# A hybrid decoder layer on one core: gates from plain one-hot columns, and mixers on four pairs of tiles

## The chip, the core and the metric

The kernel runs on one core of a Trainium2 chip. The metric is device time in microseconds (us). The kernel before took 3249.86 us, the median of 3 runs (3240.8 to 3261.46). Five engines work side by side: PE (TensorE, matmuls; its weight loads are listed apart as PEld), DVE (VectorE), ACT (ScalarE), POOL (GpSimd) and SP (SyncE, which issues most transfers). Each works through its own list of instructions in order and waits on semaphores for the others. Data moves between HBM and the on-chip SBUF by DMA; matmul results land in PSUM.

## The reference

One layer over 1024 tokens of 1024 features, all in float32, in four steps:

```
h = x
h += W_out [ norm(attn) ; norm(conv) ]     # token mixers: both from norm(h) @ w_in
h += PEER(norm(h))                         # 8 heads x 16 of 128*128 experts per token
h += sigmoid(norm(h) @ W_g) * (p @ W_p)
return norm(h)

# PEER, for a block of 128 tokens: eb = expert numbers (i1*128 + i2), gb = softmax gates
h   = einsum('td,tkd->tk', xb, expert_u[eb])
act = gelu(h) * gb
y   = einsum('tk,tkd->td', act, expert_v[eb])
```

Attention has 8 heads of 64 under three dilated causal patterns, the convolution 31 taps over 512 channels. The search for experts takes the 16 best of 128 keys on each of two sides, then the 16 best sums, for each token and head: 128 slots a token.

## The kernel before

**Tiles and groups.** The 1024 tokens are 8 tiles of 128. GROUPS cuts them into five groups: tile 0, then (1, 2), (3, 4), (5, 6), then tile 7. For each group the kernel streams all mixer and search weights once (22 MB a group): stage_in projects q, k, v; stage_attend does attention and the convolution; stage_out normalises, projects with w_out and adds the residual; stage_search projects PEER queries and finds the top keys on DVE; stage_combine finds the top sums, the gates and the expert numbers. The loop near the end of tile_layer interleaves the stages of neighbouring groups. In matmuls with channels on the partitions (channel_major) the moving operand is as wide as the group: 128 or 256 columns; in those with tokens on the partitions (token_major) each tile costs the same in any group.

**The convolution** (convolve) splits its taps: 16 go through ACT (a scaled copy, `tap`) and POOL (an add, `side`), 15 through DVE (`cc`).

**Two ways through PEER.** Four tiles (FEW: 0, 1, 2, 7) gather: for each of 128 slots, POOL issues an indirect DMA that brings each token's row of expert_u (512 KB in all) into one of 6 buffers, DVE multiplies and sums it (`hk`); then the same with expert_v (`gy`). That is 256 rows of 512 KB a tile, 1024 in all, and they run in the background of everything else. The other four tiles (ALL: 3, 4, 5, 6) are dense: after the mixers, dense walks all 16384 experts in 128 column blocks, 32 groups of 4, with hi/lo split float32 matmuls (`ph`, `py`), and needs for each token a dense row of gates.

**The gate matrix.** gate_matrix builds those rows. For each token the slots' i1, i2 and gate stand on 128 partitions, and a matmul of two one-hot matrices, one of them scaled by the gates, gives 128 x 128 gates. For each 8 tokens DVE makes `o1` (128 keys x 8 tokens, bf16), for each 4 tokens `o2` (128 keys x 4 tokens), both with the tokens innermost; the scaling is one POOL multiply for the first four tokens (`ob`) and four ACT copies for the second four (`oa`). PE multiplies (`pG`), reading columns at a stride of 4; ACT copies PSUM to `stage`, SP writes 2 MB pieces to DRAM (`gate_d`). Each float32 matmul shows as two records on PE.

**What sets the order.** A scheduler in the framework writes each engine's list in advance; gathers, which come last in the program, are placed where it sees room. Buffers decide the rest: the dense stage's v and al tiles lie where the mixers' pool was, so they wait for the last stage_combine.

## Time and profile before

| what | us |
|---|---|
| median of 3 runs | 3249.86 |
| lowest and highest run | 3240.8, 3261.46 |
| the profiled execution | 3265.54 |
| its span, first to last instruction | 3263.7 |

The profiled execution is one run, 15.7 us above the median; 1.8 us of it lie outside the span. Its stages, as the trace shows them: mixers and search from 0 to 1103 us, the gate matrix from 1103 to 1413, the last search's combine to 1444, the dense stage to about 3034, the dense tiles' last step to 3154, then the last gathers and the last tile's last step to 3264. In the rows further down, a time in a list of instructions is the start in us from the span's start, followed by the duration; "mean ns" is the mean duration of one instruction. A duration is longer than the step to the next instruction of the same engine, since neighbours overlap a little.

### The profile page before, as it was taken

The page shows a single profiled execution, that of the slowest core. Times are in us where ns is not written, and L with a number is a line of the kernel's source. Part 1 is how long each engine was busy: PE and PEld are TensorE (multiplying, and loading weights), DVE is VectorE, ACT ScalarE, POOL GpSimd, SP SyncE. Part 2 cuts the span into 40 slices and gives each one's busy share as a digit, 9 for nine tenths or more (in the row PEclk, how much of TensorE's full clock was granted, in tenths as well). Part 3 has the DMA queues.
Part 4 walks back from the last instruction along what each step waited for, and adds up shares of the span by engine and source line. Part 5 has one row for each costly group of instructions (what it writes and reads, how often), then busy time and mean ns, then how long its engine had stood idle before and what let it go on. Part 6 is the DMA issues. An engine that isn't in the chain of part 4 may idle for free.

```text
span 3263.7 us, 37043 instructions
## 1 busy us (share of the span) xinstructions
PE 2814.0 (86%) x11843; PEld 2126.9 (65%) x11843; DVE 2633.1 (81%) x5226; ACT 1198.8 (37%) x2180; POOL 1650.2 (51%) x1392
## 2 busy tenths in 40 slices
PE   6697898899797599978999999899999997999952
PEld 3454375476366399965777777577777775777621
DVE  3379789889989766686888888778988886889895
ACT  4445326335525467752222222322222223222321
POOL 1247646353544443324565556545655554555673
PEclk9898999899899699989999999999999999999976
DMA  6575982684495363369999999989999998999895
GB/s 204 177 277 192 345 327 100 219 326 146 130 340 179 135 232 144 154 241 330 345 347 339 324 335 331 340 300 339 335 336 328 335 318 318 329 350 330 323 344 199
DMA packets 299989, 901.47 MB, mean 276 GB/s; under 512 B 27866, under 2 KB 94834, under 8 KB 297746
## 3 DMA queue, kind: packets, MB, share of 16 engines
q0 software_dynamic: 147456, 536.94, 45.6%
q1 hardware_dynamic: 149072, 358.81, 31.3%
q10 hardware_dynamic: 3266, 3.36, 0.3%
q8 instruction: 93, 1.52, 0.2%
q14 instruction: 102, 0.84, 0.1%
HBM read 857.06 MB, written 41.94 MB: 275 GB/s over the span
## 4 chain that ended last, share of the span: by engine, by line
PE 33%; DVE 25%; DMA 16%; issue 15%; POOL 8%; ACT 3%; ACTq 0%; POOLq 0%; SPq 0%; DVEq 0%
PE pG L674 7%; DMA v<-in_expert_v_dram 5%; POOL v L593 4%; DVE cc L356 4%; DVE gy L622 3%; DMA v<-in_expert_v_dram,ex 3%; DVE u L606 3%; PE py L760 2%; PE py L762 2%; PE py L761 2%; PE pq L270 2%; DVE ul L707 2%; POOL u L593 2%; PE o L261 2%; PE kept_y L760 2%
## 5 line engine op out<-in xcount | busy, mean ns | idle before, releaser
L593 POOL DMA_INDIRECT u<-in_expert_u_dram,ex x512 | 672.9, 1314 | 679.3 <-DVE hk L606 428.2
L593 POOL DMA_INDIRECT v<-in_expert_v_dram,ex x512 | 663.6, 1296 | 552.3 <-DVE gy L622 381.1
L622 DVE SCALAR_TENSOR_TENSOR gy<-v,ga,gy 128x1024 f32<-128x1024 f32 x512 | 663.8, 1296 | 50.3 <-DMA v<-in_expert_v_dram,ex 41.8
L606 DVE CUSTOM_DVE_ANT_0 u<-u,gxn 128x1024 f32<-128x1024 f32 x512 | 613.8, 1230 | 33.6 <-DMA u<-in_expert_u_dram,ex 32.3
L731 PE MATMUL ph<-xh,ul 128*128 128x512 f32 x1024 | 407.6, 398 | 24.9 <-DVE ul L707 24.5
L729 PE MATMUL ph<-xh,uh 128*128 128x512 f32 x1024 | 404.1, 395 | 14.8 <-ACT uh L705 14.8
L730 PE MATMUL ph<-xl,uh 128*128 128x512 f32 x1024 | 403.8, 394 | 0.0
L747 ACT CAST vh<-v 128x1024 fp32r<-128x1024 f32 x128 | 131.5, 1049 | 645.3 <-PE py L762 420.5
L350 POOL TENSOR_TENSOR side<-side,tap 128x256 f32<-128x256 f32 (+1 forms) x300 | 216.9, 724 | 174.1 <-ACT tap L349 152.6
L760 PE MATMUL py<-vh,ah 128*128 128x512 f32 x640 | 257.4, 403 | 51.9 <-ACT ah L739 51.9
L270 PE MATMUL pq<-x2T,w_pq 128*128 128x256 f32 (+1 forms) x1280 | 247.6, 343 | 12.4 <-ACT xt L286 5.7
L761 PE MATMUL py<-vl,ah 128*128 128x512 f32 x640 | 255.1, 401 | 0.0
L762 PE MATMUL py<-vh,al 128*128 128x512 f32 x640 | 253.7, 403 | 0.0
L731 PEld LDWEIGHTS ph<-xh,ul 128*128 128x128 f32 x1024 | 194.1, 190 | 79.5 <-DVE ul L707 37.6
L270 PEld LDWEIGHTS pq<-x2T,w_pq 128*128 128x128 f32 x1280 | 214.9, 195 | 36.1 <-ACT xt L286 6.1
L729 PEld LDWEIGHTS ph<-xh,uh 128*128 128x128 f32 x1024 | 194.2, 190 | 57.7 <-ACT uh L705 15.0
L749 DVE TENSOR_TENSOR vl<-v,vh 128x1024 fp32r<-128x1024 f32 x128 | 155.1, 1221 | 88.2 <-ACT vh L747 85.9
L730 PEld LDWEIGHTS ph<-xl,uh 128*128 128x128 f32 x1024 | 193.9, 189 | 43.6 <-issue 2.4
L705 ACT CAST uh<-u 128x1024 fp32r<-128x1024 f32 x128 | 134.4, 1050 | 135.2 <-PE ph L730 93.3
L760 PEld LDWEIGHTS py<-vh,ah 128*128 128x128 f32 x640 | 122.0, 191 | 90.7 <-ACT ah L739 64.6
L663 POOL TENSOR_TENSOR ob<-o,gT 128x512 f32<-128x512 bf16 x64 | 96.6, 1509 | 165.2 <-PE pG L674 142.1
L739 ACT CAST ah<-gelu 128x512 fp32r<-128x512 f32 x128 | 79.2, 620 | 273.3 <-DVE gelu L737 270.4
(262 smaller groups left out, 5358.4 us busy)
## 6 DMA issues: line engine op xcount, KB each, us to landing
u<-in_uT_dram SPq DMA_DIRECT2D x128, 512.0 KB
v<-in_expert_v_dram SPq DMA_DIRECT2D x128, 512.0 KB
w_pq<-in_peer_wq_dram SPq DMA_DIRECT2D x80, 512.0 KB
gate_d<-stage SPq DMA_DIRECT2D x16, 2048.0 KB
gt<-gate_d SPq DMA_DIRECT2D x64, 512.0 KB
w_o<-in_w_out_dram SPq DMA_DIRECT2D x40, 512.0 KB
we<-in_w_ple_gate_dram SPq DMA_DIRECT2D x24, 512.0 KB
w_k<-in_w_qkv_dram SPq DMA_DIRECT2D x20, 512.0 KB
```

The source lines that it names most:

```text
L270: nc.tensor.matmul(a, w[:, k, :], xT[:, k, :], start=k == 0, stop=k == KD - 1)
L350: G.tensor_tensor(side, side, m, ALU.add)
L593: d = G.indirect_dma_start(out=e, out_offset=None, in_=table, in_offset=bass.IndirectOffsetOnAxis(ap=index, axis=0))
L606: uses(V.tensor_tensor_reduce(out=e, in0=e, in1=xn, scale=1.0, scalar=0.0, op0=ALU.mult, op1=ALU.add, accum_out=hk[:, k : k + 1]))
L622: uses(V.scalar_tensor_tensor(y, e, act[:, k : k + 1], y, ALU.mult, ALU.add))
L674: nc.tensor.matmul(pg[:, rows(e)], o2[:, :, e], parts[e], start=True, stop=True)
L729: nc.tensor.matmul(ph, hi, xh[:, k, :], start=k == 0, stop=False)
L730: nc.tensor.matmul(ph, hi, xl[:, k, :], start=False, stop=False)
L731: nc.tensor.matmul(ph, lo, xh[:, k, :], start=False, stop=k == KD - 1)
L760: nc.tensor.matmul(py, ah[e][:, rows(j)], vh[e][:, half(f)], start=first, stop=False)
L761: nc.tensor.matmul(py, ah[e][:, rows(j)], vl[e][:, half(f)], start=False, stop=False)
L762: nc.tensor.matmul(py, al[e][:, rows(j)], vh[e][:, half(f)], start=False, stop=last_e)
```

## The change

The groups become four pairs, (0, 1), (2, 3), (4, 5), (6, 7); the gathered tiles are now 0, 1, 6, 7 and the dense ones 2 to 5. In the gate matrix o1, ob and the iotas table go. o2 is laid out with each token's 128 columns side by side; and for each token one instruction compares the key numbers with i1 and multiplies by the gate, on DVE for even tokens and on POOL for odd ones. ACT no longer scales anything there. A scratch tile of rstd moves to the buffers t2, and the search results get a fourth buffer.

```diff
-GROUPS = ((0,), (1, 2), (3, 4), (5, 6), (7,))
+GROUPS = ((0, 1), (2, 3), (4, 5), (6, 7))
-VB = 3
+VB = 4
-FEW = (0, 1, 2, 7)
-ALL = (3, 4, 5, 6)
+FEW = (0, 1, 6, 7)
+ALL = (2, 3, 4, 5)
...
-            sq = junk(f"sqj_{name}_{j}") if junk else mpool.tile([P, D], BF16, tag="sqj", name=f"sqj_{name}_{j}")
+            sq = junk(f"sqj_{name}_{j}") if junk else mpool.tile([P, D], BF16, tag="t2", name=f"sqj_{name}_{j}", bufs=3)
...
-            for o in range(0, BT, TB):
+            for o in range(0, BT, 4):
                 t0 = b * BT + o
-                o1 = gp.tile([P, NK, TB], BF16, tag="o1", name=f"o1_{j}_{t0}", bufs=2)
-                V.tensor_tensor(o1, i1T[:, t0 : t0 + TB].unsqueeze(1).to_broadcast([P, NK, TB]), iotas, ALU.is_equal)
-                for h in range(0, TB, 4):
-                    o2 = gp.tile([P, NK, 4], F32, tag="o2", name=f"o2_{j}_{t0 + h}", bufs=2)
-                    i2s = i2T[:, t0 + h : t0 + h + 4].unsqueeze(1).to_broadcast([P, NK, 4])
-                    V.tensor_tensor(o2, i2s, iotas[:, :, 0:4], ALU.is_equal)
-                    pg = sps(f"pG{j}_{t0 + h}")
-                    t = t0 + h
-                    if h == 0:
-                        a = gp.tile([P, NK, 4], F32, tag="ob", name=f"ob{j}_{t}")
-                        G.tensor_tensor(
-                            a, o1[:, :, 0:4], gT[:, t : t + 4].unsqueeze(1).to_broadcast([P, NK, 4]), ALU.mult
-                        )
-                        parts = [a[:, :, e] for e in range(4)]
-                    else:
-                        parts = []
-                        for e in range(4):
-                            a = gp.tile([P, NK], F32, tag="oa", name=f"oa{j}_{t}_{e}", bufs=3)
-                            S.activation(a, o1[:, :, h + e], AF.Copy, scale=gT[:, t + e : t + e + 1])
-                            parts.append(a)
-                    for e in range(4):
-                        nc.tensor.matmul(pg[:, rows(e)], o2[:, :, e], parts[e], start=True, stop=True)
-                    S.copy(stage[:, :, o + h : o + h + 4], pg.rearrange("p (t i) -> p i t", i=NK))
+                o2 = gp.tile([P, 4, NK], F32, tag="o2", name=f"o2_{j}_{t0}", bufs=3)
+                V.tensor_tensor(
+                    o2, i2T[:, t0 : t0 + 4].unsqueeze(2).to_broadcast([P, 4, NK]),
+                    iota.unsqueeze(1).to_broadcast([P, 4, NK]), ALU.is_equal,
+                )
+                pg = sps(f"pG{j}_{t0}")
+                for e in range(4):
+                    t = t0 + e
+                    a = gp.tile([P, NK], F32, tag=f"oa{e % 2}", name=f"oa{j}_{t}", bufs=4)
+                    (G if e % 2 else V).tensor_scalar(a, iota, i1T[:, t : t + 1], gT[:, t : t + 1], ALU.is_equal, ALU.mult)
+                    nc.tensor.matmul(pg[:, rows(e)], o2[:, e, :], a, start=True, stop=True)
+                S.copy(stage[:, :, o : o + 4], pg.rearrange("p (t i) -> p i t", i=NK))
```

The scheduler writes new lists from this. On DVE, early in the gate matrix, the list of before is the first one below and that of the change the second (o are the one-hot tiles, oa the scaled ones, gy the gathered sums of expert_v, xn a normalised tile).

```order
L654 TENSOR_TENSOR o_0_24_7400<-i1T_7303,iotas 128x1024
L658 TENSOR_TENSOR o_0_24_7402<-i2T_7309,iotas 128x512
L622 SCALAR_TENSOR_TENSOR gy_19722<-v_108_20048,ga_19719,gy_19722 128x1024
L658 TENSOR_TENSOR o_0_28_7412<-i2T_7309,iotas 128x512
L654 TENSOR_TENSOR o_0_32_7430<-i1T_7303,iotas 128x1024
L658 TENSOR_TENSOR o_0_32_7432<-i2T_7309,iotas 128x512
```

```order
L653 TENSOR_TENSOR o_0_0_6468<-i2T_6461,cst 128x512
L458 SCALAR_TENSOR_TENSOR xn_6410<-h_6_6340,r_ffn_6407,g_ffn 128x1024
L458 SCALAR_TENSOR_TENSOR xn_6426<-h_7_6342,r_ffn_6407,g_ffn 128x1024
L661 TENSOR_SCALAR oa_0_6471<-cst,i1T_6455,gT_6465 128x128
L661 TENSOR_SCALAR oa_2_6477<-cst,i1T_6455,gT_6465 128x128
L653 TENSOR_TENSOR o_0_4_6484<-i2T_6461,cst 128x512
```

From there DVE's list repeats one o and two oa, 128 times, with nothing between; gathers, the last search and the dense input stand behind the whole gate matrix. In the list of before they were mixed in. And the first o now stands behind both output projections of the last group (rows h_6, h_7 are read by the xn above).

POOL's list at the same place, before and with the change:

```order
L663 TENSOR_TENSOR ob_88_7633<-o_0_88_7628,gT_7313 128x512
L663 TENSOR_TENSOR ob_96_7663<-o_0_96_7658,gT_7313 128x512
L593 DMA v_119_20081<-in_expert_v_dram,ex_1462 128x1024
L663 TENSOR_TENSOR ob_104_7691<-o_0_104_7686,gT_7313 128x512
L593 DMA v_120_20084<-in_expert_v_dram,ex_1462 128x1024
```

```order
L592 DMA v_97_19624<-in_expert_v_dram,ex_1845 128x1024
L592 DMA v_98_19627<-in_expert_v_dram,ex_1845 128x1024
L661 TENSOR_SCALAR oa_1_6474<-cst,i1T_6455,gT_6465 128x128
L661 TENSOR_SCALAR oa_3_6480<-cst,i1T_6455,gT_6465 128x128
L661 TENSOR_SCALAR oa_5_6490<-cst,i1T_6455,gT_6465 128x128
```

The 256 oa of POOL now follow each other without a gather between them.

The end of DVE's list, from the last scaling of a dense tile's output on, before and with the change (v_77 and v_56 are numbers of slots; the last slot is 127 in both):

```order
L804 SCALAR_TENSOR_TENSOR h_6_5846<-h_6_5846,r_fin_19328,g_fin 128x1024
L622 SCALAR_TENSOR_TENSOR gy_22338<-v_77_22571,ga_22335,gy_22338 128x1024
L622 SCALAR_TENSOR_TENSOR gy_22338<-v_78_22574,ga_22335,gy_22338 128x1024
L622 SCALAR_TENSOR_TENSOR gy_22338<-v_79_22577,ga_22335,gy_22338 128x1024
L622 SCALAR_TENSOR_TENSOR gy_22338<-v_80_22580,ga_22335,gy_22338 128x1024
```

```order
L792 SCALAR_TENSOR_TENSOR h_5_4678<-h_5_4678,r_fin_18937,g_fin 128x1024
L621 SCALAR_TENSOR_TENSOR gy_21947<-v_56_22117,ga_21944,gy_21947 128x1024
L621 SCALAR_TENSOR_TENSOR gy_21947<-v_57_22120,ga_21944,gy_21947 128x1024
L621 SCALAR_TENSOR_TENSOR gy_21947<-v_58_22123,ga_21944,gy_21947 128x1024
L621 SCALAR_TENSOR_TENSOR gy_21947<-v_59_22126,ga_21944,gy_21947 128x1024
```

51 gathered rows stood behind the last dense tile, now 72 do. Counted along DVE's list, 255 gathered rows stood ahead of the last combine's end, now 232; in between, in the dense stage, both lists hold 20 rows for each group of four column blocks, and 28 to 34 where a gathered tile's last step falls in.

## Rows read from the trace of the kernel before

**Rows 1.** The page: span, busy time of each engine, and the mean busy share of the 16 DMA engines in 40 equal slices (tenths).

```profile
span 3263.7 us, 37043 instructions
PE 2814.0 (86%) x11843; PEld 2126.9 (65%) x11843; DVE 2633.1 (81%) x5226; ACT 1198.8 (37%) x2180; POOL 1650.2 (51%) x1392
DMA  6575982684495363369999999989999998999895
```

**Rows 2.** Busy time by stretch: from:to in us, length, then busy us and number of instructions of PE, PEld, DVE, ACT, POOL, the granted PE clock (share of full speed), DMA share, GB/s.

```profile
0.00:170.00 170.00, 111.67 (x584) 77.02 (x584) 57.59 (x247) 75.16 (x179) 28.11 (x64) 0.90 0.59 193
170.00:300.00 130.00, 112.12 (x433) 68.00 (x434) 112.34 (x306) 72.38 (x161) 76.19 (x74) 0.93 0.63 224
300.00:569.00 269.00, 230.35 (x941) 153.04 (x939) 232.46 (x682) 117.47 (x242) 163.74 (x152) 0.93 0.72 262
569.00:850.00 281.00, 249.52 (x1050) 164.20 (x1050) 252.51 (x814) 122.54 (x244) 129.34 (x125) 0.93 0.59 212
850.00:1103.00 253.00, 185.60 (x842) 125.86 (x842) 227.76 (x698) 106.30 (x220) 107.75 (x126) 0.87 0.57 204
1103.00:1413.00 310.00, 302.15 (x1389) 290.54 (x1389) 203.72 (x373) 210.58 (x448) 124.65 (x86) 0.96 0.48 178
1413.00:1444.00 31.00, 16.36 (x61) 12.68 (x62) 30.54 (x105) 8.59 (x10) 3.88 (x4) 0.72 0.73 252
1444.00:3034.00 1590.00, 1476.43 (x6150) 1162.07 (x6149) 1340.17 (x1843) 435.55 (x578) 881.05 (x652) 0.98 0.93 331
3034.00:3154.00 120.00, 107.43 (x344) 61.98 (x343) 105.71 (x109) 40.88 (x84) 82.36 (x67) 0.94 0.95 350
3154.00:3230.00 76.00, 0.00 (x0) 0.00 (x0) 65.89 (x52) 1.01 (x2) 53.13 (x46) 0.50 0.92 337
3230.00:3264.00 34.00, 22.40 (x56) 11.51 (x56) 4.37 (x7) 8.32 (x19) 0.00 (x0) 0.80 0.04 15
```

**Rows 3.** Groups of matmuls on PE up to 1430 us, shapes apart: busy us, mean ns of one record, idle before them. Busy time counts each moment once, so busy by number is the pace of a record.

```profile
L270 PE MATMUL pq<-x2T,w_pq 128*128 128x256 f32 x768 | 174.0, 384 | 10.1 <-ACT xt L286 5.7 <-DMA w_pq<-in_peer_wq_dram 3.0 <-issue 0.8
L674 PE MATMUL pG<-ob,o 128*128 128x128 f32 x512 | 149.8, 437 | 2.3 <-POOL ob L663 2.0
L674 PE MATMUL pG<-oa,o 128*128 128x128 f32 x512 | 136.1, 391 | 0.0
L261 PE MATMUL o<-w_o,yT 128*128 128x512 f32 x256 | 132.5, 669 | 16.0 <-DMA w_o<-in_w_out_dram 14.8 <-ACT yT L167 1.2
L270 PE MATMUL pq<-x2T,w_pq 128*128 128x128 f32 x512 | 73.7, 280 | 2.3 <-DMA w_pq<-in_peer_wq_dram 1.7 <-ACT pqT L480 0.5
```

**Rows 4.** Groups of DVE instructions, shapes apart: the second one-hot tile and the gathered sums that fall into the gate matrix (1103 to 1413 us), and the nearest kin of the new instruction, a two-scalar operation on 128x128 in the convolution (up to 1430 us).

```profile
L658 DVE TENSOR_TENSOR o<-i2T,iotas 128x512 f32<-128x512 bf16 x128 | 88.6, 692 | 81.2 <-PE pG L674 78.0 <-PE pq L270 3.0
L622 DVE SCALAR_TENSOR_TENSOR gy<-v,ga,gy 128x1024 f32<-128x1024 f32 x22 | 35.1, 1596 | 0.1
...
L353 DVE TENSOR_SCALAR cc<-glu,cw 128x128 f32<-128x128 f32 x8 | 3.2, 406 | 0.0
```

**Rows 5.** Groups of POOL instructions: the gate multiply (up to 1430 us), and the convolution's add on 128x128 in the first group (50 to 110 us).

```profile
L663 POOL TENSOR_TENSOR ob<-o,gT 128x512 f32<-128x512 bf16 x64 | 96.6, 1509 | 165.2 <-PE pG L674 142.1 <-PE pt_xw L687 5.8 <-ACT yc L413 5.2
...
L350 POOL TENSOR_TENSOR side<-side,tap 128x128 f32<-128x128 f32 x60 | 27.9, 466 | 76.0 <-ACT tap L349 71.9
```

**Rows 6.** DVE in order of time, in the convolution of the third pair: start, duration. POOL's convolution adds run until shortly after 860 us.

```profile
858.79 0.94 DVE L356 SCALAR_TENSOR_TENSOR cc<-glu,cw,cc 128x256 f32<-128x256 f32 x1
...
860.53 0.47 DVE L356 SCALAR_TENSOR_TENSOR cc<-glu,cw,cc 128x256 f32<-128x256 f32 x1
```

**Rows 7.** PE in order of time: the last gate matmuls of the first group (one tile) and of the second (a pair), start and end of the search's matmuls for one tile (the k row follows it) and for a pair.

```profile
71.96 1.95 PE L270 MATMUL a<-xT,w_a 128*128 128x128 f32 x16
...
129.33 6.65 PE L270 MATMUL pq<-x2T,w_pq 128*128 128x128 f32 x48
...
169.99 1.12 PE L261 MATMUL k<-w_k,xT 128*128 128x512 f32 x2 [0.46 <-ACT xT L167]
...
271.68 3.62 PE L270 MATMUL a<-xT,w_a 128*128 128x256 f32 x16
...
417.45 10.53 PE L270 MATMUL pq<-x2T,w_pq 128*128 128x256 f32 x48
...
485.77 2.97 PE L270 MATMUL pq<-x2T,w_pq 128*128 128x256 f32 x13
```

**Rows 8.** DVE in order of time: the convolution of the three pairs of before, late in each pair's share of DVE.

```profile
289.42 9.15 DVE L356 SCALAR_TENSOR_TENSOR cc<-glu,cw,cc 128x256 f32<-128x256 f32 x12
...
559.56 10.47 DVE L356 SCALAR_TENSOR_TENSOR cc<-glu,cw,cc 128x256 f32<-128x256 f32 x12
...
840.81 10.03 DVE L356 SCALAR_TENSOR_TENSOR cc<-glu,cw,cc 128x256 f32<-128x256 f32 x12
```

**Rows 9.** DVE behind the gate matrix: one of the five search instructions (all of up to 1430 us), the dense input (up to 1430 us), and the end of the last combine in order of time.

```profile
L492 DVE FIND_INDEX8 idxs<-vals,sc 128x8 uint32<-128x128 f32 x128 | 35.2, 286 | 0.0
...
L683 DVE SCALAR_TENSOR_TENSOR xw<-h,r_wide,g_ffn 128x1024 f32<-128x1024 f32 x4 | 8.3, 2064 | 0.0
...
1443.46 0.31 DVE L579 SCALAR_TENSOR_TENSOR ex<-i,i 128x128 int32<-128x128 bf16 x1
```

**Rows 10.** DVE in order of time: the first and the last of the 51 gathered sums behind the last dense tile.

```profile
3154.38 5.24 DVE L622 SCALAR_TENSOR_TENSOR gy<-v,ga,gy 128x1024 f32<-128x1024 f32 x4
...
3225.03 3.93 DVE L622 SCALAR_TENSOR_TENSOR gy<-v,ga,gy 128x1024 f32<-128x1024 f32 x3 [0.77 <-DMA v<-in_expert_v_dram,ex]
```

More of the change, by code (lines that the diff above doesn't have):

```diff
@@ L53 @@
 BT = 32
-TB = 8
 LAG = 5
@@ L636, in gate_matrix @@
         tr = []
-        for what, src, dt in (("i1", i1, BF16), ("i2", i2, BF16), ("g", gate, F32)):
+        for what, src in (("i1", i1), ("i2", i2), ("g", gate)):
             f = flat(src)
-            if dt != F32:
+            if what != "g":
                 f32 = mpool.tile([P, SLOTS], F32, tag="t2", name=f"gl{what}{j}", bufs=3)
@@ L644, in gate_matrix @@
             nc.tensor.transpose(pt[:, 0:P], f, ident)
-            d = gp.tile([P, P], dt, tag=f"{what}T", name=f"{what}T{j}", bufs=2)
+            d = gp.tile([P, P], F32, tag=f"{what}T", name=f"{what}T{j}", bufs=2)
             S.copy(d, pt[:, 0:P])
@@ L864, in tile_layer @@
     gph, gp = scope(ctx, name="gph", side="right")
-    iotas = gp.tile([P, NK, TB], BF16, name="iotas")
-    V.tensor_copy(iotas, iota.unsqueeze(2).to_broadcast([P, NK, TB]))
     h1 = dict(zip(sum(GROUPS, ()), sum((h1s[g] for g in range(NG)), [])))
```

## The prediction

> **What bounds the kernel now.** I read the page first, then the busy time by stretch, then the groups of the stretches that the change touches, at last the lists in time. The page shows no single bound: PE is busy 86%, DVE 81%, and the DMA engines are full in the second half only [rows 1]. The stretches say why [rows 2]. The mixers, to 1103 us, are DVE's and PE's together: in the two middle stretches DVE is busy 232 of 269 and 253 of 281 us, PE 230 and 250. The gate matrix, 1103 to 1413, is PE's: 302 of 310 us. The dense stage, to 3034, moves 331 GB/s with the DMA engines 93% busy and PE 93% (1476 of 1590). Behind 3154 only gathered rows of the last tile arrive, and 34 us of its last step follow. So a microsecond saved ahead of the dense stage is kept only if no gathered rows are put off to the end for it.
>
> **The mixers.** The loop has one round less, but the same eight tiles go through it.
>
> *The first pair.* For tile 0 alone the second group's k began at 170 us [rows 7]. A pair adds: three token-major projections for one more tile, 3 x 16 records at 132.5/256 = 0.52 us, 25 us; channel-major ones with 256 columns, 3.62 against 1.95 us per 16 records, eight times, 13 us; the output projection, 32 records, 17 us; the search, 72 us (417 to 489) against 41 (129 to 170), 31 us [rows 3, 7]. The convolution's extra adds lie beside these. Sum 86; with a few us of normalising, the second group begins at about 260 us.
>
> *The rounds.* From there I go by DVE, which finished its share of the second, third and fourth group at about 299, 570 and 851 us (the end of each row's run) [rows 8]: 129 us after the k of 170, then 271, then 281. With the change the first share has a second combine (about 20 us, below) and four more gathered rows by the list: 155, so 415. The second has tiles 4 and 5 in attention instead of 3 and 4, I add 10: 696. The third holds 90 gathered rows by the list instead of 66; 24 at 1.3 us are 31 us [rows 10], of which the 28 us that DVE stood idle there may hide a few [rows 2]; with 25 added, 306: 1002. Before, one more round with a single tile followed, and the gate matrix began at 1103 beside its output projection. The list now puts the gate matrix behind both output projections of a pair: 64 records at 0.52 us, 33 us [rows 3], the rest of the last combine, 20, and some 12 for the two normalisations, 65 us: 1067, I say **1070**. That is **33 us** earlier, though a whole group of weights (22 MB) is not read any more: those reads lay beside DVE and PE, with the DMA engines busy 57 to 72% [rows 2].
>
> **The gate matrix.** Its price is now that of the slowest of four engines for 128 units of four tokens.
>
> *PE.* Strided columns go; contiguous ones of the same shape run at 73.7/512 = 0.144 us a record against 0.28 now [rows 3]. Eight records a unit are 1.15 us, 147 in all; with 47 of the last search's matmuls that the list sets between (94 records at 174/768 = 0.23, 21 us) and a few transposes, 174 us. That is the floor.
>
> *ACT.* Its 256 scalings go; what is left, a copy a unit, needs less than PE. Nothing, hidden under DVE and PE.
>
> *DVE.* One o2, 0.69 (0.60 from start to start), and two of the new instruction, whose nearest kin took 0.41 [rows 4], 0.25 from start to start where nothing disturbs it (an estimate from that row). Together 1.10 us a unit.
>
> *POOL.* Two of the new instruction a unit. No row shows it on POOL. Bounds: its add of the same size, 0.47 us; and the gate multiply, 1.51 us for four times the elements [rows 5]. I take the add, which has the size.
>
> *Between DVE and POOL.* In the convolution, where both have work without a pause, a DVE instruction took 0.94 us while POOL was adding and 0.47 when POOL had ended [rows 6]: it waited for about one POOL instruction. In the gate matrix of before, o2 kept its 0.69 beside POOL's multiplies [rows 4]. Now both have work without a pause, as in the convolution. If two of DVE's three wait 0.25 to 0.3 us, a unit takes 1.65 us; the ends are 1.10 (none wait, then PE's 1.36 decides) and, with all waits whole, 1.10 + 2 x 0.47 = 2.03. With **1.65** the stage takes **211 us**, to 1281. The Trainium skill, page "SBUF — State Buffer", section "Who interferes with whom", says that a DVE instruction with two SBUF inputs, or in a two-port mode, and a GpSimd instruction that reads SBUF exclude each other, the later blocked whole; the row of the convolution agrees, the o2 of before does not show it. By that rule the unit is the 2.03 above.
>
> *Behind it.* DVE's list puts the search of two tiles, the dense input, two combines and 11 gathered rows there, where before one search was spread under PE's 310 us. A search is 16 lists of five instructions of at most 0.286 us [rows 9], 23 us, two 46. A combine: the 30.5 us to 1443.5 less about eight other instructions [rows 2, 9], 20 to 21; two 42. The dense input 8.3 and about 5 us; the gathered rows 14 [rows 9, 10]. About 115, and the first splits of the dense stage: **119 us**, to **1400** against 1443.5. PE has its rest of the search done by then and waits. Gain so far 44 us. In the stretch between, POOL's 22 gathered rows that cost DVE 35 us [rows 4] are gone; they come back below.
>
> On SP the order is the same in kind: weight pieces of the last search behind 2 MB gate writes, 16 of each; at 178 GB/s [rows 2] before, and some 250 now, they stay hidden. The scratch tile in t2 may wait for a search tile now and then; the fourth result buffer takes such a wait away. Both at nothing, up to 5 us.
>
> **The dense stage.** Both lists give 20 gathered rows to each group of four blocks. The stage is at the DMA engines' rate, and its bytes are the same: no change, at most 2 us gained by matmuls done ahead.
>
> **The end.** 72 gathered rows instead of 51 stand behind the last dense tile. The 51 took 3154.4 to 3229, 1.46 us each [rows 10]; 21 more are **31 us**, with nothing beside them, since PE stands still there [rows 2].
>
> **Sum.** -33 (mixers) -11 (gate matrix and what follows, 330 us against 340.5) +31 (end) = -13 us on the profiled execution's 3265.5, hence 3252; its run lay 15.7 above the median, so **3237 us** as a median: no change that can be told. What a measurement of this kernel can tell from none is about 1%, 32 us, hence 3217 and 3282.
>
> **Rivals.**
> - *DVE and POOL hardly disturb each other* (for it: o2 kept its 0.69 [rows 4]). PE's 174 us decide, 37 less: 3200; if the rounds also close up by 20 us, 3180. Chance 0.30.
> - *Each blocks the other whole* (for it: 0.94 against 0.47 [rows 6]). The unit takes 2.03, 260 us, 49 more: 3286. Chance 0.12.
> - *POOL's instruction itself is long, so the kernel gets slower.* Two scalars a partition and two operations in one instruction are in no row of POOL; at the 1.3 us that lie between the add and the gate multiply [rows 5] POOL alone needs 2.6 us a unit, 333 us: 3359. It decides from a unit of 1.75 us, where nothing is gained; at 2.0, a POOL instruction of a full us, it is over 1% slower. Chance 0.12.
> - *The pairs shorten nothing*: the first gather starts some 90 us later, the third round is fuller, and the gate matrix begins at 1103 as before: 3270. Chance 0.08.
> - The forecast, within 25 us either way: 0.38.
>
> **Chances.** Faster by over 1%: most of the first rival and a fifth of the forecast's spread, 0.36. Slower by over 1%: the long instruction, half of the whole blocking and some of the rest, 0.23. Between: 0.41. The range, **3165 to 3310**, takes in all but the long POOL instruction and the best of the first rival; the forecast's own range is 3212 to 3262.
>
> **What the profile will show.** The second group's k near 260 us; the first pG near 1075; pG records at 0.145 us busy and no idle PE if the first rival holds, else DVE back to back with o2 well above 0.69 or oa above 0.41, and POOL's oa near 0.5; the last ex near 1400; 20 rows a group in a dense stage as long as before; and 105 us instead of 75 between the last dense tile and the last tile's step. The prediction is wrong in its main step if POOL's instruction is over 0.8 us or DVE's unit under 1.4, and in its last if the rows at the end do not cost 1.46 us each.

## The result, and the profile after

The changed kernel takes **3289.64 us**, the median of 4 runs (3283.25 to 3290.74), beside 3245.33 for the kernel before (4 runs, 3239.99 to 3261.46): 1.011 times as long, with a 95% interval of 1.008 to 1.0141. Measured once more beside the last runs it came to 1.0085 (1.0054 to 1.0115). It is about 1% slower. The profiled execution took 3289.18 us, 23.6 more than that of the kernel before.

The page of the changed kernel: the span, the engines' busy time, and the groups of the gate matrix (busy us, mean ns | idle before them), which answer to [rows 1, 3, 5].

```profile
span 3287.4 us, 35738 instructions
PE 2696.0 (82%) x11459; PEld 1981.4 (60%) x11459; DVE 2656.6 (81%) x5336; ACT 1036.9 (32%) x1813; POOL 1786.6 (54%) x1524
...
L661 POOL TENSOR_SCALAR oa<-cst,i1T,gT 128x128 f32<-128x128 f32 x256 | 259.8, 1029 | 0.0
...
L662 PE MATMUL pG<-oa,o 128*128 128x128 f32 x1024 | 176.7, 296 | 66.7 <-POOL oa L661 62.1
...
L662 PEld LDWEIGHTS pG<-oa,o 128*128 128x128 f32 x1024 | 138.5, 191 | 106.0 <-POOL oa L661 103.2
```

POOL's 256 `oa` are a new group, 1029 ns each and with no idle time before them. PE, whose `pG` records were 437 and 391 ns long, has them at 296; its busy time for 1024 falls from 286 to 177 us. But PE and its weight loads now wait for POOL.

The busy time by stretch, with the columns of [rows 2]: first pair, gate matrix, what stands behind it, dense stage, the last rows.

```profile
0.00:279.00 279.00, 207.93 (x796) 138.31 (x797) 116.33 (x465) 105.76 (x241) 46.16 (x64) 0.90 0.39 126
...
1086.00:1350.00 264.00, 195.73 (x1166) 155.06 (x1167) 176.93 (x393) 87.93 (x167) 262.22 (x258) 0.99 0.36 147
1350.00:1460.00 110.00, 69.52 (x334) 57.09 (x332) 108.79 (x481) 22.20 (x37) 12.04 (x10) 0.84 0.46 151
1460.00:3028.00 1568.00, 1450.68 (x6114) 1144.24 (x6115) 1341.02 (x1833) 438.87 (x579) 879.99 (x654) 0.99 0.94 337
...
3150.00:3254.00 104.00, 0.00 (x0) 0.00 (x0) 91.21 (x71) 0.57 (x1) 75.90 (x66) 0.50 0.94 349
```

Against [rows 2]: the gate matrix begins at 1086 instead of 1103, takes 264 instead of 310, and then 110 us follow in place of 31. The last `ex` (the expert numbers, with which the last combine ends) comes at 1460.2 instead of 1443.5, **17 us later**. The last rows take 104 us instead of 76, **30 us more** with the edges. That is 47 us, and the medians lie 44 apart. The dense stage is shorter by 22 us in these two profiles, which is why the profiled executions lie only 23.6 apart; the last two runs below tell what that is.

### The profile page after: what moved, and what is told of

Same layout as the page of the kernel before. It is cut to its first block, busy times and chain, and to the rows that moved or that the text cites. A ratio compares the mean times of both kernels' runs of the same rounds, so it can differ in the third digit from the quotient of the medians.

```text
span 3287.4 us, 35738 instructions
## 1 busy us (share of the span) xinstructions
PE 2696.0 (82%) x11459; PEld 1981.4 (60%) x11459; DVE 2656.6 (81%) x5336; ACT 1036.9 (32%) x1813; POOL 1786.6 (54%) x1524
## 4 chain that ended last, share of the span: by engine, by line
PE 28%; DVE 25%; issue 17%; POOL 15%; DMA 12%; ACT 2%; POOLq 0%; ACTq 0%; SPq 0%; DVEq 0%
POOL oa L661 6%; POOL v L592 6%; DMA v<-in_expert_v_dram 4%; DVE cc L355 3%; PE o L260 3%; DVE u L605 3%; POOL u L592 3%; DVE gy L621 3%; DMA v<-in_expert_v_dram,ex 3%; PE plg L782 2%; PE pq L269 2%; DMA u<-in_expert_u_dram,ex 2%; DVE ul L695 2%; PE s L374 2%; PE py L748 2%
## 5 line engine op out<-in xcount | busy, mean ns | idle before, releaser
L592 POOL DMA_INDIRECT u<-in_expert_u_dram,ex x512 | 662.0, 1293 | 685.8 <-DVE hk L605 421.3
L621 DVE SCALAR_TENSOR_TENSOR gy<-v,ga,gy 128x1024 f32<-128x1024 f32 x512 | 656.6, 1282 | 58.4 <-DMA v<-in_expert_v_dram,ex 49.4
L349 POOL TENSOR_TENSOR side<-side,tap 128x256 f32<-128x256 f32 x240 | 195.4, 815 | 188.7 <-ACT tap L348 173.4
L661 POOL TENSOR_SCALAR oa<-cst,i1T,gT 128x128 f32<-128x128 f32 x256 | 259.8, 1029 | 0.0
L269 PE MATMUL pq<-x2T,w_pq 128*128 128x256 f32 x1024 | 238.3, 383 | 2.6 <-DMA w_pq<-in_peer_wq_dram 2.6
L662 PE MATMUL pG<-oa,o 128*128 128x128 f32 x1024 | 176.7, 296 | 66.7 <-POOL oa L661 62.1
L269 PEld LDWEIGHTS pq<-x2T,w_pq 128*128 128x128 f32 x1024 | 189.9, 192 | 27.6 <-ACT pqT L479 2.5
L662 PEld LDWEIGHTS pG<-oa,o 128*128 128x128 f32 x1024 | 138.5, 191 | 106.0 <-POOL oa L661 103.2
```

The costliest lines, as they stand in the source:

```text
L269: nc.tensor.matmul(a, w[:, k, :], xT[:, k, :], start=k == 0, stop=k == KD - 1)
L592: d = G.indirect_dma_start(out=e, out_offset=None, in_=table, in_offset=bass.IndirectOffsetOnAxis(ap=index, axis=0))
L621: uses(V.scalar_tensor_tensor(y, e, act[:, k : k + 1], y, ALU.mult, ALU.add))
L661: (G if e % 2 else V).tensor_scalar(a, iota, i1T[:, t : t + 1], gT[:, t : t + 1], ALU.is_equal, ALU.mult)
L662: nc.tensor.matmul(pg[:, rows(e)], o2[:, e, :], a, start=True, stop=True)
```

## The experiments

Two theories stood at the start. *POOL's instruction*: it needs 1.03 us and sets the gate matrix by itself, at 2.05 us a unit of four tokens; DVE is not slowed. *The exclusion*: DVE and POOL stop each other and only seem not to. To the second the groups on DVE in the changed kernel answer (up to 1450 us):

```profile
L661 DVE TENSOR_SCALAR oa<-cst,i1T,gT 128x128 f32<-128x128 f32 x256 | 91.4, 358 | 7.2 <-PE pG L662 1.5
L653 DVE TENSOR_TENSOR o<-i2T,cst 128x512 f32<-128x512 f32 x128 | 88.7, 693 | 76.9 <-PE pG L662 76.5 <-ACT i2T L645 0.3
```

`o` with 693 ns is as long as it was beside POOL's multiplies [rows 4]; DVE's idle time is a wait for PE, and PE waits for POOL.

### One instruction in four on POOL, and none

```diff
-(G if e % 2 else V).tensor_scalar(...)
+V.tensor_scalar(...)                      # none
+(G if e == 3 else V).tensor_scalar(...)   # one
```

None:

> All four compare-and-multiply instructions of a unit on DVE, none on POOL. Theory (POOL's instruction alone costs 1.03 us and two of them set the unit of 2.05 us; DVE was never slowed): DVE decides with 0.60 for o2 and 4 x about 0.27 for oa, 1.7 us a unit, about 215 us between the first and the last pG in place of 263; PE waits for DVE. With some 7 gathered rows more behind the last dense tile (10 us) the time is about 3250 us, 1.2% under the changed kernel. Rival (the unit is held by something that both engines share, such as the result buffers or the waits between DVE and PE): taking POOL away does not shorten the unit, it stays at 2.0 us or longer, and the time at 3290 or above.

One:

> Three of four compare-and-multiply instructions on DVE, one on POOL. Theory: POOL needs 1.03 us a unit and no longer decides; DVE 0.60 + 3 x 0.27 = 1.4 us and PE about 1.36 us lie level, so the unit is 1.4 to 1.5 us, 180 to 192 us for the stage in place of 263, and with 10 us more at the end the time is about 3220 us. Rival (DVE and POOL exclude each other when both have work without a pause, and DVE only looked undisturbed because it waited for PE): DVE's oa or o2 gets longer by about half a microsecond where POOL's instruction stands beside it, the unit is 1.9 us or more, and the time 3280.

Measured: none 3256.53 us, 1.0017 of before (0.9985 to 1.0048); one **3230.92 us, 0.9917 (0.989 to 0.9945)**, faster than both kernels. The stages take 213 us, 1.66 a unit, and 181 us, 1.41 a unit. Groups of the gate matrix, on DVE with none on POOL, then on POOL and DVE with one:

```profile
L661 DVE TENSOR_SCALAR oa<-cst,i1T,gT 128x128 f32<-128x128 f32 x512 | 141.9, 338 | 0.6 <-PE pG L662 0.5
L653 DVE TENSOR_TENSOR o<-i2T,cst 128x512 f32<-128x512 f32 x128 | 87.3, 682 | 0.3 <-ACT i2T L645 0.3
```

```profile
L661 POOL TENSOR_SCALAR oa<-cst,i1T,gT 128x128 f32<-128x128 f32 x128 | 175.8, 1386 | 2.8 <-PE pG L662 2.7
...
L661 DVE TENSOR_SCALAR oa<-cst,i1T,gT 128x128 f32<-128x128 f32 x384 | 118.4, 367 | 0.7 <-PE pG L662 0.6
...
L653 DVE TENSOR_TENSOR o<-i2T,cst 128x512 f32<-128x512 f32 x128 | 88.0, 687 | 0.1
```

Taking work from POOL and giving it to DVE shortens the stage by 51 and by 83 us, so POOL set it. The time falls by less: the lists leave 148 gathered rows behind the last vl (DVE's split of a block of expert_v, the last of 128 in the dense stage) where the changed kernel's leaves 140, and from that vl to the last row pass 246 and 247 us in place of 230. DVE has next to no idle time in either. Its two instructions grow by 5 and 29 ns where POOL works beside it: DVE pays almost nothing here. POOL's one instruction, however, got longer, 1386 ns. The first theory had a number for its length and no reason for it.

### All four on POOL, and POOL with one operation

```diff
-(G if e % 2 else V).tensor_scalar(...)
+G.tensor_scalar(...)                                            # all four
+G.tensor_scalar(a, iota, i1T[:, t : t + 1], None, ALU.is_equal) # odd tokens, one operation
```

> All four compare-and-multiply instructions on POOL, DVE has only o2. Theory (the 1.03 us are the instruction's own): POOL's oa keeps a mean near 1.0 us, the unit is 4.1 us and the gate matrix takes about 525 us, 262 more than in the changed kernel, and DVE fills some of that with search and gathered rows, so the time is 3480 to 3550 us. Rival (the 1.03 us come from DVE's instructions beside it): with DVE's 0.69 us in 4 the mean falls to 0.5 to 0.7 us, the unit to 2.0 to 2.8 us.

> POOL's instruction has one operation and one scalar a partition (the comparison alone; the gate is left out of the odd tokens' columns), all else as in the changed kernel. If it is the second operation with its second scalar that makes POOL's instruction long: its mean falls to about 0.5 us, the unit to 1.4 to 1.6 us, the stage to 180 to 205 us. If a comparison or a scalar a partition is slow on POOL by itself: it stays near 1.0 us, and stage and time stay at 263 and 3290 us. I hold the first for a little likelier.

Measured: 3479.35 us and 3243.17 us, one run each. POOL's instructions, min/median/max in ns, in the changed kernel, with all four on POOL, and with one operation:

```profile
L661 POOL TENSOR_SCALAR oa<-cst,i1T,gT x256: 787/974/2617, 1088.8 to 1347.8; 128x128 f32<-128x128 f32 x128
```

```profile
L661 POOL TENSOR_SCALAR oa<-cst,i1T,gT x512: 782/789/3332, 1086.8 to 1592.3; 128x128 f32<-128x128 f32 x171
```

```profile
L662 POOL TENSOR_SCALAR oa<-cst,i1T x256: 594/812/1330, 1082.1 to 1300.4; 128x128 f32<-128x128 f32 x128
```

All four: the stage is near what the first theory had, 507 us (3.96 a unit) where 525 were expected, but the mean falls to 892 ns, on the way to the rival's 0.5 to 0.7 us. One operation: a mean of 869 ns and a stage of 220 us (1.72 a unit), between the two cases. With DVE almost quiet the median is 789 ns, next to the changed kernel's minimum of 787: that is the instruction's own length, and the rest of the 1029 is not its own. With one operation it is 594, so the second operation with its scalar costs 0.2 us, not half.

### Who lengthens POOL's instruction

By then the excess over 0.79 was 0.48 us a unit in the changed kernel, where DVE works 1.1 us a unit, and 0.60 with one instruction on POOL, where DVE works 1.4: about 0.43 for each us of DVE. Two runs put that to the test.

```diff
-(G if e % 2 else V).tensor_scalar(...)
+for _ in range(1 if e % 2 else 3): (G if e % 2 else V).tensor_scalar(...)  # three times
...
+for _ in range(2): V.tensor_tensor(o2, ...)   # o2 twice, and for even tokens a = iota
```

> The changed kernel, with each of DVE's two compare-and-multiply instructions of a unit made three times (the same result written again), so that DVE has 0.60 + 6 x 0.265 = 2.2 us of work a unit instead of 1.1; POOL's two are as before. Theory (POOL's instruction takes 0.79 us by itself and loses about 0.43 us for each us that DVE works beside it): POOL needs 1.58 + 0.43 x 2.2 = 2.5 us a unit, still decides, its mean rises to 1.25 us and the stage to 320 us. Rival (the 1.03 us are a length of their own, and the 1.39 us seen with one POOL instruction a unit hold a wait for DVE's step): DVE decides with 2.2 us, 280 us for the stage, and POOL shows idle time or a mean of at most 1.1 us.

> The changed kernel without DVE's compare-and-multiply (the even tokens are multiplied with the table of key numbers instead, so their gates are left out), and with o2 made twice, so that DVE has 1.2 us a unit in o2 alone. If every DVE instruction takes its share from POOL: POOL's mean stays at 1.0 to 1.05 us, the unit at 2.1, the stage at 260 to 270 us. If only the compare-and-multiply of DVE does: POOL's mean falls to 0.79 us, the unit to 1.6, the stage to about 205 us. By the all-POOL run, where o2 itself grew from 0.68 to 0.86 us, I hold something between for possible, nearer to the first.

Measured: 3349.94 and 3314.73 us, one run each. The first has 2.2 us a unit, DVE without a pause, and 282 us for the stage; the second 315 us, 2.46 a unit. POOL's groups up to 1400 us (7 instructions of the second run stand behind):

```profile
L662 POOL TENSOR_SCALAR oa<-cst,i1T,gT 128x128 f32<-128x128 f32 x256 | 279.5, 1104 | 4.9 <-PE pG L663 4.6
```

```profile
L663 POOL TENSOR_SCALAR oa<-cst,i1T,gT 128x128 f32<-128x128 f32 x249 | 294.8, 1195 | 1.9 <-PE pG L666 1.6
```

The 2.5 us and 320 us of the first run's theory did not come; DVE's rate and POOL's mean are the rival's. But the second run lies above both of its expectations, and the rival has no room for that. The share for each us of DVE is no constant: six compare-and-multiplies of DVE hardly lengthened POOL's two, and two o2 alone lengthened them more, by 0.81 us a unit, than the whole of DVE's work in the changed kernel, 0.48. The single instructions in order of time say why (start, duration). With o2 twice:

```profile
1199.69 0.69 DVE L654 TENSOR_TENSOR o<-i2T,cst 128x512 f32<-128x512 f32 x1 [1.24 <-PE pG L666]
1199.87 2.21 POOL L663 TENSOR_SCALAR oa<-cst,i1T,gT 128x128 f32<-128x128 f32 x1
1200.30 0.68 DVE L654 TENSOR_TENSOR o<-i2T,cst 128x512 f32<-128x512 f32 x1
1200.90 0.68 DVE L654 TENSOR_TENSOR o<-i2T,cst 128x512 f32<-128x512 f32 x1
1202.07 0.79 POOL L663 TENSOR_SCALAR oa<-cst,i1T,gT 128x128 f32<-128x128 f32 x1
1202.66 0.69 DVE L654 TENSOR_TENSOR o<-i2T,cst 128x512 f32<-128x512 f32 x1 [1.08 <-PE pG L666]
1202.84 1.18 POOL L663 TENSOR_SCALAR oa<-cst,i1T,gT 128x128 f32<-128x128 f32 x1
```

The POOL instruction that meets three o2 in a row takes 2.21 us, 1.42 more than its 0.79; the one that meets one takes 1.18; the one between takes 0.79. With DVE's other instruction three times:

```profile
1199.70 0.68 DVE L653 TENSOR_TENSOR o<-i2T,cst 128x512 f32<-128x512 f32 x1
1199.78 1.36 POOL L662 TENSOR_SCALAR oa<-cst,i1T,gT 128x128 f32<-128x128 f32 x1
1200.30 0.33 DVE L662 TENSOR_SCALAR oa<-cst,i1T,gT 128x128 f32<-128x128 f32 x1
1201.12 0.87 POOL L662 TENSOR_SCALAR oa<-cst,i1T,gT 128x128 f32<-128x128 f32 x1
```

1.36 beside o2 and compare-and-multiplies, 0.87 beside compare-and-multiplies. And the changed kernel itself:

```profile
1188.36 0.69 DVE L653 TENSOR_TENSOR o<-i2T,cst 128x512 f32<-128x512 f32 x1 [0.49 <-PE pG L662]
1188.54 1.31 POOL L661 TENSOR_SCALAR oa<-cst,i1T,gT 128x128 f32<-128x128 f32 x1
1188.97 0.34 DVE L661 TENSOR_SCALAR oa<-cst,i1T,gT 128x128 f32<-128x128 f32 x1
1189.36 0.34 DVE L661 TENSOR_SCALAR oa<-cst,i1T,gT 128x128 f32<-128x128 f32 x1
1189.84 0.79 POOL L661 TENSOR_SCALAR oa<-cst,i1T,gT 128x128 f32<-128x128 f32 x1
1190.43 0.69 DVE L653 TENSOR_TENSOR o<-i2T,cst 128x512 f32<-128x512 f32 x1 [0.72 <-PE pG L662]
1190.61 1.18 POOL L661 TENSOR_SCALAR oa<-cst,i1T,gT 128x128 f32<-128x128 f32 x1
```

The two that begin while an o2 runs take 1.31 and 1.18; the one between, which meets only the start of the next o2, takes 0.79. **A POOL instruction that begins while a DVE instruction that reads two tensors runs stands still until that one ends. Those of DVE that read one tensor and scalars cost it about 0.1 us** (0.87 against 0.79 with three times as many of them). It holds for a gathered sum too, which reads two tensors (all four on POOL). There POOL's instruction begins while an o2 runs, and the sum follows the o2 at once:

```profile
1299.25 0.87 DVE L653 TENSOR_TENSOR o<-i2T,cst 128x512 f32<-128x512 f32 x1 [2.32 <-PE pG L662]
1299.91 1.91 POOL L661 TENSOR_SCALAR oa<-cst,i1T,gT 128x128 f32<-128x128 f32 x1
1300.04 1.28 DVE L621 SCALAR_TENSOR_TENSOR gy<-v,ga,gy 128x1024 f32<-128x1024 f32 x1
```

The unit of 2.05 is therefore 2 x 0.79 for POOL's own work and 0.48 for one o2. With one instruction on POOL it is 0.79 + 0.60, which DVE's own 1.4 covers.

**Who waits is settled by who begins first.** In the changed kernel 118 of the 128 o2 begin in the last 0.2 us of a POOL instruction. They keep 0.69 us, that POOL instruction keeps its 0.79, and the next one, which begins 0.18 us behind the o2's start, is held: in the rows above it ends 0.67 and 0.80 us behind the o2's end, nearly its whole own length. With all four on POOL 102 of the 128 o2 begin 0.10 to 0.15 us into a POOL instruction instead, and there DVE pays:

```profile
1200.32 0.78 POOL L661 TENSOR_SCALAR oa<-cst,i1T,gT 128x128 f32<-128x128 f32 x1
1200.44 0.86 DVE L653 TENSOR_TENSOR o<-i2T,cst 128x512 f32<-128x512 f32 x1 [3.13 <-PE pG L662]
1201.10 0.87 POOL L661 TENSOR_SCALAR oa<-cst,i1T,gT 128x128 f32<-128x128 f32 x1
```

The o2 takes 0.17 us more than its 0.69, the POOL instruction that came first keeps its 0.78, and the next one, which begins 0.2 us ahead of the o2's end, loses 0.09. What decides where in a POOL instruction the o2 begins was not tested.

### The groups apart from the gate matrix

The pairs with the gate matrix of before; and the five groups of before with the gate matrix of the changed kernel, once with one instruction in four on POOL and once as changed.

```diff
-GROUPS = ((0, 1), (2, 3), (4, 5), (6, 7))      # VB, FEW and ALL likewise
+GROUPS = ((0,), (1, 2), (3, 4), (5, 6), (7,))
```

> The four pairs with the gate matrix of before, strided columns and all; only the scratch tile of the squares shares t2 as in the changed kernel. Theory (the pairs by themselves move little: the gate matrix starts 17 us earlier, its 302 us of PE come back, and two searches instead of one stand behind or in it): the last ex near 1450 us, as many rows at the end as before (120 behind the last vl by the list), time within 0.5% of before. Rival (the pairs are what makes the changed kernel slower): 1.0 to 1.5% slower than before, with 20 rows more at the end.

> The gate matrix of the run with one POOL instruction in four, but the tiles in the five groups of before (0 | 1, 2 | 3, 4 | 5, 6 | 7; tiles 0, 1, 2 and 7 gathered, tile 0 alone first). Theory (what counts is how many gathered rows are done ahead of the last dense tile; the tile that starts alone lets them begin 100 us earlier): the list puts 276 rows ahead of the last ex in place of 225; the gate matrix starts at 1120 to 1160 us, takes 181 again, the last ex comes near 1390, the rows behind the last dense vl fall from 148 to 97, 50 x 1.5 us less, and the time is 3170 to 3200 us, 0.97 to 0.985 of before. Rival (the pairs save their round: a group of weights less, the gate matrix 17 us earlier): it is slower than the pairs with the same gate matrix, 3245 us or more, 0.996 to 1.0 of before.

> The gate matrix exactly as changed (two of four instructions on POOL), with the five groups of before. Theory (the two parts add up: two POOL instructions in four instead of one cost 2.0% with the pairs, 1.011 against 0.992, and will cost the same with five groups): 0.981 x 1.0195 = 1.000 of before, 3255 to 3265 us beside a before of 3258; POOL's instruction near 1.03 us, the unit near 2.05, the stage 255 to 265 us. Rival (POOL's time only matters where the pairs leave two searches behind the gate matrix, which would otherwise fill DVE's idle time): 0.985 to 0.99 of before.

Measured, as ratios to before with 95% intervals:

| | gate matrix of before | as changed, two on POOL | one on POOL |
|---|---|---|---|
| five groups | 1 | 1.0077 (1.0051 to 1.0103) | **0.9813** (0.9787 to 0.9839) |
| four pairs | 1.0006 (0.9984 to 1.0029) | 1.011 and 1.0085 | 0.9917 (0.989 to 0.9945) |

The pairs alone move nothing, as expected; the gate matrix as written costs 0.8% without them. **So the slowdown is the gate matrix's.** With one instruction on POOL and five groups the kernel takes 3200.29 us, the best seen here and faster than both kernels. That is the upper edge of what was expected, and its path was not: the gate matrix began at 1202 us instead of 1120 to 1160, and the last ex came at 1439 instead of 1390. In this run the gate matrix begins behind the last group's output projection, whose last record starts at 1197; before, that one started at 1122 and the gate matrix, at 1103, ahead of it. The time expected for the five groups with two on POOL was missed: from one to two costs 2.7% there and not 2.0%. With five groups the two lists hold the same rows (276 ahead of the last ex, 97 behind the last vl), so the whole of the stage's 89 us shows. With the pairs the list of two on POOL leaves 140 rows behind the last vl and that of one 148, and 230 us pass from there to the last row instead of 247, which gives 17 us back. With five groups and two on POOL, POOL's mean is 1049 ns and its instructions take 265 us, as expected.

How the pairs break even, by stretches of the run with the gate matrix of before (gate matrix, what follows):

```profile
1075.00:1376.00 301.00, 298.33 (x1318) 289.32 (x1319) 199.74 (x364) 210.72 (x443) 127.85 (x90) 0.98 0.48 179
1376.00:1460.00 84.00, 42.37 (x183) 33.95 (x181) 82.93 (x345) 15.27 (x21) 13.29 (x9) 0.78 0.47 166
```

The gate matrix begins some 28 us earlier than in the profile of before and takes its 300 us again, but 83 us of DVE follow where 31 did [rows 2]; the last ex comes at 1459.4, and 120 rows stand behind the last vl as before.

Why five groups beat the pairs by 1% with the fast gate matrix, and not with the others, is only half answered. The last ex comes 72 us later, 1439.0 against 1366.5; from the last vl to the last gathered row pass 168 us and not 247, for 97 rows and 148. That makes 7 us. Of the 29 us between the two profiled executions 18 more lie between the first and the last vl, a time that differs by 10 and 23 us between two runs of one program (below). This stays open.

### Half of the first pair's convolution

```diff
-for k in range(SIDE_TAPS + 1, TAPS):
+for k in range(SIDE_TAPS + 1, TAPS, 1 if g else 2):   # POOL's taps likewise
```

> The changed kernel, with every second tap of the convolution left out for the first pair, on DVE (28 adds of 0.75 us, 21 us) and on POOL (28 to 32 adds): the first pair's tiles are computed with half their taps. Theory (the first pair's k came 19 us later than predicted because the convolution's adds of twice the width stand on its path, with PE idle for them): the second group's k begins 17 to 22 us earlier, at 257 to 262 us, the first pG about as much earlier, near 1070, and the last ex likewise. Rival (the adds lie beside the projections, and the lower granted clock or the weights hold PE there): the second group's k stays within 5 us of 279.

Measured: 3256.49 us. The second group's k on PE, in order of time, in the changed kernel and in this run:

```profile
278.76 2.08 PE L260 MATMUL k<-w_k,xT 128*128 128x512 f32 x2 [0.46 <-ACT xT L166]
```

```profile
256.30 2.08 PE L260 MATMUL k<-w_k,xT 128*128 128x512 f32 x2 [0.46 <-ACT xT L166]
```

22.5 us earlier, a little more than the 17 to 22 expected; the first pG 33.8 earlier, at 1057.5, and the last ex 33, for which 17 to 22 were expected too. The 11 us more stay open; a second run of the changed kernel (below) has its first pG 4.5 us earlier than the first run had. Taps are left out on DVE and on POOL, so the run does not part the two. Two groups of the changed kernel say the same: DVE's adds (40 to 201 us), and what PE waited for (100 to 201 us).

```profile
L355 DVE SCALAR_TENSOR_TENSOR cc<-glu,cw,cc 128x256 f32<-128x256 f32 x56 | 41.8, 752 | 1.3
```

```profile
L421 PE MATMUL pc<-cst,cc 128*128 128x128 f32 x8 | 2.6, 399 | 19.5 <-DVE cc L356 17.4 <-DVE glu L334 1.2 <-ACT sg L330 0.9
```

The 752 ns are not the width alone. An add of this width with no POOL instruction beside it takes 0.47 us (the median of 41 in the changed kernel, and the second of [rows 6]). Of the 56, 39 took 0.74 us or more, and 38 of these began while a POOL instruction ran. By this reckoning 56 x 0.47 = 26 of the 42 us are the adds' own and 16 are waiting for POOL: the exclusion again, with DVE as the one that comes second. No run tests that apart.

### Both kernels once more

> The changed kernel once more, beside the other runs. If the dense stage's 1546 us from the first to the last vl (1572 in the profile of before) belong to the program, they come again within 5 us; if the stage varies from run to run, it lies anywhere from 1545 to 1575. The ratio to before: 1.008 to 1.014 again.

> The kernel before once more, for a second profile of it. If the dense stage of before is long by itself, the first to the last vl take 1567 us or more again. If the 1572 us came from that one run, whose time lay 15 to 20 us over the median, they take 1545 to 1560 and the run about 3245 us.

Measured: 3285.14 us (7 runs, ratio above) and 3250.16 (one run). The dense stage from the first to the last vl (first and last start in the middle of the line):

```profile
L737 DVE TENSOR_TENSOR vl<-v,vh x128: 1210/1218/1228, 1472.6 to 3028.1; 128x1024 fp32r<-128x1024 f32 x128
```

```profile
L749 DVE TENSOR_TENSOR vl<-v,vh x128: 1210/1218/1281, 1463.3 to 3012.4; 128x1024 fp32r<-128x1024 f32 x128
```

1555.5 and 1549.1 us, where the first profiles had 1546.0 and 1572.3. The same program differs by 10 and 23 us, so the 22 us that the dense stage seemed to gain belong to one long run of before, and its 20 rows a group changed nothing. The end is steady: from the last vl to the last row the kernel before takes 200.3 and 200.1 us, the changed kernel 230.2 and 228.9.

## Why the prediction was wrong

**The step that failed is POOL's term in the gate matrix**, with what was said of DVE and POOL. The prediction gave POOL's instruction 0.47 us, "the add, which has the size", and let DVE wait for POOL: a unit of 1.65, 211 us. The instruction takes 0.79 by itself, and it is POOL that waits, 0.48 us a unit, for DVE's o2: 2 x 0.79 + 0.48 = 2.05, 263 us. Neither alone would have done it: 2 x 0.79 is 1.58 and 2 x 0.47 + 0.48 is 1.42, both under the 1.65. By the prediction's own sign, a POOL instruction of over 0.8 us, its main step is wrong: 1.03 stand in the profile. The rows held a warning for the first half: an instruction with two operations was bounded by 0.47 and 1.51, and the value lay between. For the second half the row used, o2 keeping its 0.69 beside POOL [rows 4], was read as the absence of contention. It shows only that DVE does not pay there. POOL's side was in the same trace, in the gate multiply `ob` [rows 5]. DVE and POOL in the kernel before, two places:

```profile
1200.14 0.69 DVE L658 TENSOR_TENSOR o<-i2T,iotas 128x512 f32<-128x512 bf16 x1 [0.20 <-PE pG L674]
1200.24 1.49 POOL L663 TENSOR_TENSOR ob<-o,gT 128x512 f32<-128x512 bf16 x1
...
1384.83 0.69 DVE L658 TENSOR_TENSOR o<-i2T,iotas 128x512 f32<-128x512 bf16 x1 [0.27 <-PE pG L674]
1385.22 1.20 POOL L663 TENSOR_TENSOR ob<-o,gT 128x512 f32<-128x512 bf16 x1 [3.98 <-PE pG L674]
```

59 of the 64 began 0.1 us behind the start of an o2 and took 1.49, like the first. The one that began 0.39 us behind it took 1.20. Both end 0.90 us behind the o2's end, so the 1.51 held a wait for it.

**Two rivals had the size**, neither with the mechanism. Whole blocking gave 2.03 and 3286; the long POOL instruction said "at 2.0, a POOL instruction of a full us, it is over 1% slower". The first had the wrong engine waiting and 0.47 for POOL's instruction, so that its 3286 lies near the measured 3290 is luck; the second took the whole length for the instruction's own. The row of the convolution [rows 6] from which the blocking was taken has an add of POOL beside it that is 256 columns wide and took 1.05 us (858.40 us): DVE waited 0.47 us of it, not for all of it. The Trainium skill, page "SBUF — State Buffer", section "Who interferes with whom", says that a DVE instruction with two SBUF inputs and a GpSimd instruction that reads SBUF exclude each other, and one with a single input outside the two-port modes does not. The runs agree on the first pair, 1.31 us for POOL's instruction beside an o2; in which mode DVE's oa run no run shows, and they cost POOL about 0.1 us. On who pays, that section of the Trainium skill has the later one blocked, whichever it is. The runs agree in the main: the POOL instruction that began during an o2 waited, and with all four on POOL the o2 that began 0.12 us into a POOL instruction grew, to a median of 862 ns against 682. But that o2 lost 0.17 us and not the 0.66 that POOL's instruction still ran, and at 1190.43 us an o2 that began in the last 0.2 us of one kept its 0.69. POOL's instruction, as the profile records it, does not hold DVE over its whole length.

**The mixers** gained 17 us and not 33. The first pair is the error: k at 278.8, predicted 260. "The convolution's extra adds lie beside these" was wrong; 56 adds of 0.75 us in place of 56 of 0.41 stand on the path with PE idle, and halving them, with POOL's, gave back 22.5 us. Of their 42 us some 16 are waiting for POOL, by the reckoning above, so this term too failed in part on what the two engines cost each other. From there to the gate matrix the prediction had 810 us and the trace has 807.

**Behind the gate matrix** 119 us were predicted and 111 measured, **the end** 105 and 105 (72 rows at 1.46), **the dense stage** unchanged, which holds within its spread. PE's records, 0.145 predicted, took 177/1024 = 0.173 busy with waits between them.

**Where the gain of the faster columns went.** PE's 110 us were real but did not bound the stage any more, as POOL did. And before, PE's 302 us had hidden 204 us of DVE's work, a search and 22 gathered rows among it [rows 2, 4]; now DVE waited 77 us for PE in the stage, and the search and the rows stood behind it or at the end.

Summed on the profiled run, without the dense stage's 22 us: -17 (gate matrix begins) +34 (gate matrix and what follows, 374 against 340.5) +30 (end) = +47, where the prediction had -33, -11 and +31. Of the difference of 60 us, 44 are the middle term: 52 more in the gate matrix, less 8 behind it.

## What to carry to other kernels

When two engines are to share a loop, price each one's instruction alone and beside the other's; an instruction that keeps its length beside another engine may be the one that takes the time, so look at both. In this kernel DVE's instructions that read two tensors and POOL's held each other up, and the one that began second waited; DVE's that read one tensor and scalars cost POOL little. What moves to POOL should stand beside the latter, and little should move. A stage that one engine bounds hides work of the others: before it is made faster, list what it hides, since that work is laid bare.

## What the chip showed unexpectedly

POOL's compare-and-multiply on 128x128 float32 with two scalars a partition took 0.79 us, the comparison alone 0.59, DVE's same instruction 0.34. PE's granted clock over the gate matrix was 0.98 with one instruction on POOL and 0.99 in the changed kernel. With all four on POOL it was 0.51, close to the lower of its two levels (1.2 GHz), while PE did two records for each of POOL's instructions; POOL, busy 499 of 507 us, still set the stage:

```profile
1087.00:1594.00 507.00, 431.80 (x1139) 277.69 (x1140) 167.95 (x194) 88.61 (x164) 498.57 (x553) 0.51 0.32 115
```
